# Differential heads' values and probabilities as plain float32, the joint's rows one after another, later residual loads and earlier weight sums in a decoder layer

## The chip, the cores and the metric

One Trainium2 chip, one of its cores. The metric is the device time of one execution in microseconds (us), as the median of several runs. PE is TensorE, DVE is VectorE, ACT is ScalarE, POOL is GpSimd, and SP is the engine whose queue issues every DMA of this kernel.

## The reference, cut to what matters

One decoder layer over 1024 tokens and 1024 channels, all float32. A common input projection feeds 4 differential heads and 8 sparse ("NSA") heads; both results go through one output projection, a first layer norm, a SwiGLU feed-forward of width 2816 and a second layer norm.

```python
s = einsum('bqhcd,bkhcd->bhcqk', q_blk, k) * scale - slopes * dist     # two score maps, c = 0, 1
p = masked_softmax(s, dist >= 0)
a = p[:, :, 0] - lam * p[:, :, 1]
o_diff = einsum('bhqk,bkhe->bqhe', a, v)                              # v has 128 columns per head
mix = concatenate([o_diff, o_nsa]) @ w_out
x = layer_norm(ALPHA * x + mix, ln1_g, ln1_b)
ffn = (silu(x @ w_gate) * (x @ w_up)) @ w_down
x = layer_norm(ALPHA * x + ffn, ln2_g, ln2_b)
```

## The kernel before, in words

**Numbers in two halves.** A float32 matrix product is made of products of the type float32r. An operand is split into a high part (ACT casts it, L80) and a low part (DVE or POOL subtracts, L82); `mm3` (L115 to L117) adds high-high, high-low and low-high products into one PSUM bank of 512 columns. Transpositions on PE (L329, L483, L848) and the small products of the compression (L206) are plain float32.

**Attention.** Work is cut into units: one head (differential) or head pair (NSA) and one block `i` of 128 queries, so a unit has `i + 1` blocks of 128 keys. A unit's *front* makes scores on PE (L303, L304) into one of two PSUM banks `psS`, DVE scales them and takes the row's extreme (L307), ACT takes the exponential (L320), and DVE (L443 to L446) and POOL (L448, L449) combine the two maps. Its *back* transposes the result (L329) in groups of up to four blocks into `psT`, splits each group into high and low parts (`pt`, L80 and L82) and multiplies it with the values (L462, L464) into the only bank `psO`. The values of a differential head lie as 256 columns, high and low beside each other; each of the two products takes all 256, so the result has two halves of 128 columns, which ACT copies (L468) and DVE adds (L469); ACT squares the sum (L470). After four units `finish` scales the rows, transposes them (L483), and writes them to `mix_d` in DRAM (L486, L488).

**Fillers.** The table `phases` puts projections (`qf`, `kf`, `qdf`, `kdf`, `dvf`), weight loads (`wo_fill`) and the first output rows (`out_fill`) between the units; `pump` gives them out in proportion to the units' cost. `dvf(pair, blocks)` makes the values of two heads; for pair 1 it stands in the phases of heads 0 and 1. A scheduler then orders each engine's instructions by these priorities and by its own idea of what is ready. Engines work in that order, one instruction behind the other.

**The joint.** Output rows 4 to 7 (`out_half_now`, two halves of 24 products) and their layer norms run between attention and feed-forward. `x_put` transposes a finished row block and splits it into the feed-forward's moving operands; `x_sums(i)` forms the sums and differences (L864, L865, L867) of blocks `i - 4` and `i` for a seven-product scheme. The order is written out by hand: half 0 of rows 6 and 7, half 1 of row 6, the norm of row 6, half 1 of row 7, and so on. The norm takes DVE, POOL and ACT in turn, except for row 7, which is on DVE but for the root.

**Gate, up and down.** Eleven steps `p` of a pair of gate tiles and a pair of up tiles, 7 x 12 products each. `hidden_operands(p)` writes seven combinations of the hidden rows to `a_d`, `down_weights(p)` reads two weight rows into slots 11 and 9, forms four combinations on DVE and writes seven blocks to `t_d`. `down_weights(p - 1)` is called in step `p`, and that of the last pair after the loop. The down projection then runs seven passes (numbers 1, 2, 6, 5, 3, 7, 4) over 11 operands. `down_operand` loads each from `a_d` and `t_d` (L1051, L1052) into one of 16 places, and splits it; an operand serves 12 products. `residual` (L1073) loads the rows of the first norm back from `x1_d`, and `norm_params(ln2)` (L596) the second norm's scale and shift.

Of the kernel before, what the change touches and what calls it, by code (L numbers as in the profile page):

```python
# [11 lines left out]
F32 = mybir.dt.float32  # L12
F32R = mybir.dt.float32r
# [4 lines left out]
P = 128  # L18
# [20 lines left out]
def layer_kernel(ctx: ExitStack, tc: tile.TileContext, xT, x, w_t, w_vg, w_dv, lam_in, subln,  # L39
# [103 lines left out]
    with ExitStack() as ctx_a:  # L143
# [177 lines left out]

        def pt_tile():
            return pa.tile([P, 1024], F32R, tag="pt", name="pt", bufs=3)

# [99 lines left out]
        def diff_units(h, qt, kd, V):  # L424
# [3 lines left out]
            def make(i):  # L428
# [22 lines left out]
                def back(fill):  # L451
                    if i4 == 0:
                        state["orow"] = small([P, 4, P], "od", 2)
                        state["ss"] = small([P, 4], "ss", 2)
                    orow, ss = state["orow"], state["ss"]
                    po = ps_o()
                    for j4 in range(0, i + 1, 4):
                        js = range(j4, min(j4 + 4, i + 1))
                        pt = transposed([ts[0][:, j * P:(j + 1) * P] for j in js])
                        for n, j in enumerate(js):  # L460
                            v = V[j // 2][:, (j % 2) * 512 + (h % 2) * 256:(j % 2) * 512 + (h % 2 + 1) * 256]
                            nc.tensor.matmul(po[:, :256], lhsT=pt[:, 0, n * P:(n + 1) * P], rhs=v,  # L462
                                             start=(j == 0), stop=False)
                            nc.tensor.matmul(po[:, :256], lhsT=pt[:, 1, n * P:(n + 1) * P], rhs=v,  # L464
                                             start=False, stop=(j == i))
                        fill((j4 + len(js)) / (i + 1))
                    tmp = small([P, P], "ms", 2)
                    nc.scalar.copy(tmp, po[:, 128:256])  # L468
                    nc.vector.tensor_add(orow[:, i4, :], po[:, 0:128], tmp)  # L469
                    nc.scalar.activation(tmp, orow[:, i4, :], AF.Square, accum_out=ss[:, i4:i4 + 1])  # L470
                    if i4 == 3:
                        late.append(lambda: finish(orow, ss, state["r0", hf]))
# [57 lines left out]

        def dv_fill(pair, where, out, blocks):
            def steps():
                parts = [(*load_split(w_dv[pair, :, kk, :], *w_tiles(), l_eng="pool", pieces=2), 4 * kk, 4) for kk in range(2)]
                for i in blocks:
                    if i % 2 == 0:
                        out.append(slot(where[i // 2]))
                    ps = ps_m()
                    yield from proj_rows(parts, 256, i, ps)
                    dst = out[i // 2][:, (i % 2) * 512:(i % 2 + 1) * 512].rearrange("p (h s e) -> p h s e", h=2, s=2)
                    split(ps[:, :256].rearrange("p (h e) -> p h e", h=2), dst[:, :, 0, :], dst[:, :, 1, :])  # L540
            return steps, 2.61 * len(blocks)
# [50 lines left out]

        def norm_params(src):
            lnp[:] = [slot(0, F32), slot(1, F32)]
            for n in range(2):
                nc.sync.dma_start(lnp[n], src[n].unsqueeze(0).to_broadcast([P, DM]))  # L596
# [137 lines left out]
        def dvf(pair, blocks):  # L734
            return dv_fill(pair, ((8, 9, 10, 11), (6, 7, 3, 5))[pair], vd[pair], blocks)

# [6 lines left out]
        def held_fill():  # L743
# [15 lines left out]
            (diff(0), [qdf(0, 1), dvf(1, range(4)), qdf(1, 0)], 1, 0, 1),  # L759
            (diff(1), [qdf(1, 1), dvf(1, range(4, 8)), kdf(2, 0), kdf(2, 1), qdf(2, 0)], 1, 0, 1),  # L760
            (diff(2, 0, 4), [kdf(3, 0), kdf(3, 1), qdf(3, 0)], 0, 0, 2),
            (diff(3, 0, 4), [qdf(2, 1)], 0, 0, 2),
            (diff(2, 4), [wo_fill(0), qdf(3, 1), wo_fill(1), held_fill(), out_fill(0, False), out_fill(1, False)], 0, 0, 2),
# [126 lines left out]
    for i in (6, 7):  # L890
        out_start(i)
        out_half_now(i, 0, ps_s())
    x_sums(5)
    X["22"] = (x_big(), x_big())
    out_half_now(6, 1, ps_m())
    norm1(6)
    for i in (4, 5):
        x_put("22", i, acc[i][:, HI])
    out_half_now(7, 1, ps_m())
    x_sums(6)  # L900
    norm1(7, vector_only=True)
    x_put("22", 6, acc[6][:, HI])

# [95 lines left out]
    for p in range(NF // 2):  # L999
# [3 lines left out]
        next(gate)  # L1003
        if p == 0:
            x_sums(7)
            X["T1"] = (x_big(), x_big())
            next(up)
        next(gate)
# [10 lines left out]
        if p > 0:  # L1019
            next(up)  # L1020
            down_weights(p - 1)
        next(up)
# [166 lines left out]
```

## Time and profile before

| | |
|---|---|
| runs | median 1359.04 us, 1359.03 to 1361.04, of 3 |
| the profiled execution | 1355.88 us, of which the span is 1354.2 us |
| TensorE clock granted | 0.991 of full |
| busy | PE 97%, weight loads 83%, DVE 70%, ACT 48%, POOL 35% |
| DMA | 184.17 MB, 136 GB/s over the span |

A row of the timeline has start, duration, engine, line, operation and operands; what stands in brackets is how long the engine was idle before it and who ended that. A row of the windows has, for a stretch of the span, the busy time and number of instructions of each engine, the granted clock (1.00 is full), the share of the DMA engines and GB/s. Products are pipelined and their ends are modelled: a product's row can be longer than the distance to the next one's start, which is called the pitch below. A plain float32 product shows as two rows.

### The profile page before, as it was taken

What the parts mean: (1) busy time and instruction counts of PE and PEld (TensorE: products, weight loads), DVE (VectorE), ACT (ScalarE), POOL (GpSimd) and SP (SyncE); (2) the same over time, 40 slices, a digit from 0 to 9 for tenths busy, and PEclk for the clock granted to TensorE, in tenths of its full rate; (3) what the DMA queues carried; (4) which work ended last, traced back from release to release, by engine and by line L of the source; (5) the groups of instructions that cost most, each with busy time, mean ns of one, the idle gap of its engine ahead of it and who ended that gap; (6) DMA issues with size and microseconds to landing.
All of it is one profiled execution on the core that took longest, in us unless ns stands there. A gap on an engine that the chain in (4) does not pass through costs nothing.

```text
span 1354.2 us, 20369 instructions
## 1 busy us (share of the span) xinstructions
PE 1312.3 (97%) x7018; PEld 1121.8 (83%) x7018; DVE 946.6 (70%) x1936; ACT 649.9 (48%) x1329; POOL 475.2 (35%) x468
## 2 busy tenths in 40 slices
PE   8999999999999999799989999999999999899997
PEld 6898998888899988578867888888888888688886
DVE  5546768778796757874678677767767767555588
ACT  5336567677686656743336233333333325443330
POOL 5415244343543636633631233322322322000071
PEclk9999999999999999999989999999999999999999
DMA  9312021120203226423212655545555559765641
GB/s 360 123 26 61 7 59 49 30 63 16 72 15 83 79 55 197 131 79 133 101 63 86 203 193 180 179 164 187 170 172 191 190 210 400 276 217 189 199 169 65
DMA packets 87271, 184.17 MB, mean 136 GB/s; under 512 B 10624, under 2 KB 19200, under 8 KB 87040
## 3 DMA queue, kind: packets, MB, share of 16 engines
q1 hardware_dynamic: 87168, 182.87, 41.3%
q8 instruction: 55, 0.90, 0.3%
q14 instruction: 48, 0.39, 0.1%
HBM read 117.23 MB, written 57.15 MB: 129 GB/s over the span
## 4 chain that ended last, share of the span: by engine, by line
PE 85%; DMA 6%; DVE 5%; ACT 2%; issue 1%; SPq 0%; POOLq 0%; DVEq 0%; POOL 0%; ACTq 0%
PE psM L115 10%; PE psM L116 10%; PE psM L117 9%; PE psT L329 5%; PE psS L115 5%; PE psT L115 5%; PE psS L117 5%; PE psT L117 5%; PE psS L116 5%; PE psT L116 5%; PE psS L303 3%; PE psS L304 3%; PE psO L408 2%; PE psO L406 2%; DMA big<-t_d 2%; PE psO L115 2%
## 5 line engine op out<-in xcount | busy, mean ns | idle before, releaser
L320 ACT ACTIVATE t<-t,m 128x128 f32<-128x128 f32 (+7 forms) x192 | 144.3, 752 | 52.9 <-DVE m L307 47.2
L391 POOL TENSOR_SCALAR t<-t,r,gates 128x640 f32<-128x640 f32 (+7 forms) x128 | 100.6, 788 | 156.3 <-DVE r L390 103.4
L82 DVE TENSOR_TENSOR pt<-psT,pt 128x512 fp32r<-128x512 f32 (+2 forms) x200 | 117.8, 599 | 20.0 <-ACT pt L80 18.3
L115 PE MATMUL psM<-big,w 128*128 128x512 f32 x304 | 122.6, 403 | 3.0 <-ACT w L80 2.8
L80 ACT CAST pt<-psT 128x512 fp32r<-128x512 f32 (+2 forms) x200 | 99.9, 518 | 47.7 <-PE psT L329 22.0
L116 PE MATMUL psM<-big,w 128*128 128x512 f32 x304 | 120.7, 397 | 0.0
L117 PE MATMUL psM<-big,w 128*128 128x512 f32 x304 | 120.4, 397 | 0.0
L303 PE MATMUL psS<-slot,q 128*128 128x320 f32 (+5 forms) x288 | 106.5, 371 | 8.4 <-DVE m L307 7.3
L329 PE MATMUL psT<-ident,t 128*128 128x128 f32 x672 | 107.9, 274 | 2.3 <-ACT tmp L486 1.6
L957 POOL TENSOR_TENSOR half<-half,half 128x512 f32<-128x512 f32 x22 | 32.2, 1462 | 218.5 <-ACT half L956 218.5
L304 PE MATMUL psS<-slot,q 128*128 128x320 f32 (+5 forms) x288 | 95.6, 333 | 0.0
L329 PEld LDWEIGHTS psT<-ident,t 128*128 128x128 f32 x672 | 80.1, 141 | 9.8 <-ACT tmp L486 2.1
L307 DVE CUSTOM_DVE_ANT_0 t<-psS,dsel 128x512 f32<-128x512 f32 (+5 forms) x128 | 68.3, 535 | 27.5 <-PE psS L304 24.3
L82 DVE TENSOR_TENSOR op<-op 128x1024 fp32r<-128x1024 f32 x44 | 62.7, 1432 | 35.1 <-ACT op L80 34.8
L82 DVE TENSOR_TENSOR big<-slot,big 128x1024 fp32r<-128x1024 f32 (+1 forms) x53 | 64.7, 1231 | 32.1 <-ACT big L80 32.1
L80 ACT CAST big<-slot 128x1024 fp32r<-128x1024 f32 (+1 forms) x53 | 54.1, 1034 | 54.9 <-DVE slot L949 46.4
L80 ACT CAST op<-op 128x1024 fp32r<-128x1024 f32 x44 | 45.9, 1050 | 58.1 <-DMA op<-t_d 51.9
L80 ACT CAST big<-big 128x1024 fp32r<-128x1024 f32 (+1 forms) x49 | 44.6, 913 | 57.3 <-DMA big<-t_d 47.0
L408 PE MATMUL psO<-pt,slot 128*128 128x256 f32 x264 | 71.6, 293 | 0.3 <-DVE pt L82 0.2
L406 PE MATMUL psO<-pt,slot 128*128 128x256 f32 x264 | 71.1, 287 | 0.0
L303 PEld LDWEIGHTS psS<-slot,q 128*128 128x128 f32 x288 | 54.7, 190 | 18.5 <-DVE m L307 14.2
L115 PEld LDWEIGHTS psM<-big,w 128*128 128x128 f32 x304 | 57.7, 190 | 14.1 <-ACT w L80 3.6
(364 smaller groups left out, 3970.9 us busy)
## 6 DMA issues: line engine op xcount, KB each, us to landing
a_d<-slot SPq DMA_DIRECT2D x77, 256.0 KB, 3.0
t_d<-slot SPq DMA_DIRECT2D x77, 256.0 KB, 2.3
q<-q SPq DMA_DIRECT2D x48, 256.0 KB, 3.0
slot<-in_w_up_dram SPq DMA_DIRECT2D x22, 512.0 KB, 3.8
slot<-in_w_down_dram SPq DMA_DIRECT2D x22, 512.0 KB, 4.3
op<-a_d SPq DMA_DIRECT2D x44, 256.0 KB, 3.3
op<-t_d SPq DMA_DIRECT2D x44, 256.0 KB, 3.6
big<-a_d SPq DMA_DIRECT2D x33, 256.0 KB, 2.9
```

Of the source, the lines that this page charges most:

```text
L80: nc.scalar.copy(hi, src)
L82: eng.tensor_sub(lo, src, hi.bitcast(F32))
L115: nc.tensor.matmul(acc, lhsT=ah, rhs=bh, start=first, stop=False, skip_group_check=more)
L116: nc.tensor.matmul(acc, lhsT=ah, rhs=bl, start=False, stop=False, skip_group_check=more)
L117: nc.tensor.matmul(acc, lhsT=al, rhs=bh, start=False, stop=last, skip_group_check=more)
L303: nc.tensor.matmul(ps[:, :w], lhsT=q[0], rhs=k[:, ks], start=True, stop=False)
L304: nc.tensor.matmul(ps[:, :w], lhsT=q[1], rhs=k[:, ks], start=False, stop=True)
L320: nc.scalar.activation(t[:, :width], t[:, :width], AF.Exp, bias=m, scale=-1.0, accum_out=r)
L329: nc.tensor.transpose(tp[:rows, n * P:(n + 1) * P], s, ident)
L391: nc.gpsimd.tensor_scalar(ts[a][:, :width], ts[a][:, :width], r[:, a:a + 1], gates[:, i, gc:gc + 1], op0=ALU.mult, op1=ALU.mult)
L406: nc.tensor.matmul(po[:, :256], lhsT=v, rhs=pt[:, 0, n * 256:(n + 1) * 256], start=False, stop=False)
L408: nc.tensor.matmul(po[:, :256], lhsT=v, rhs=pt[:, 1, n * 256:(n + 1) * 256], start=False, stop=last)
```

## The change

1. **Differential heads.** `transposed_whole` copies each group of transposed probabilities once (ACT, L332 of the kernel after) to float32. The values stay whole: `dv_fill` copies them with ACT alone, four blocks to a slot. One float32 product of 128 columns (L472) takes the place of L462 and L464. DVE copies the result (L476) and ACT squares it straight from PSUM (L477).
2. **Values of pair 1.** They need two slots, not four; the weights are loaded once and lie in the slots 10, 11, 3 and 5. `dvf(1, range(4, 8))` moves from the phase of head 1 to that of the first half of head 3.
3. **Joint.** Row 6 is made whole, then its norm starts, then row 7 is made whole. `x_put("22", 4 to 6)` comes after row 7's norm. In step 0 the up tile's first part is written ahead of `x_sums(7)`.
4. **Weight sums.** `down_weights(p)` is called in step `p`; step 2 makes those of 0 and 2, and nothing is left after the loop.
5. **Residual loads.** `not_before` copies one column (DVE) of a bank's evacuated sum into the tile that is to be loaded, so that the load waits for the pass before; so also for the second norm's parameters.

```diff
-                        pt = transposed([ts[0][:, j * P:(j + 1) * P] for j in js])
+                        pt = transposed_whole([ts[0][:, j * P:(j + 1) * P] for j in js])
                         for n, j in enumerate(js):
-                            nc.tensor.matmul(po[:, :256], lhsT=pt[:, 0, n * P:(n + 1) * P], rhs=v,
-                                             start=(j == 0), stop=False)
-                            nc.tensor.matmul(po[:, :256], lhsT=pt[:, 1, n * P:(n + 1) * P], rhs=v,
-                                             start=False, stop=(j == i))
+                            c = (j % 4) * 256 + (h % 2) * P
+                            nc.tensor.matmul(po[:, :P], lhsT=pt[:, n * P:(n + 1) * P], rhs=V[j // 4][:, c:c + P],
+                                             start=(j == 0), stop=(j == i))
...
-                    nc.scalar.copy(tmp, po[:, 128:256])
-                    nc.vector.tensor_add(orow[:, i4, :], po[:, 0:128], tmp)
-                    nc.scalar.activation(tmp, orow[:, i4, :], AF.Square, accum_out=ss[:, i4:i4 + 1])
+                    nc.vector.tensor_copy(orow[:, i4, :], po[:, :P])
+                    nc.scalar.activation(tmp, po[:, :P], AF.Square, accum_out=ss[:, i4:i4 + 1])
...
-            (diff(1), [qdf(1, 1), dvf(1, range(4, 8)), kdf(2, 0), kdf(2, 1), qdf(2, 0)], 1, 0, 1),
+            (diff(1), [qdf(1, 1), kdf(2, 0), kdf(2, 1), qdf(2, 0)], 1, 0, 1),
-            (diff(3, 0, 4), [qdf(2, 1)], 0, 0, 2),
+            (diff(3, 0, 4), [qdf(2, 1), dvf(1, range(4, 8))], 0, 0, 2),
...
     for i in (6, 7):
         out_start(i)
-        out_half_now(i, 0, ps_s())
+    for nh in range(2):
+        out_half_now(6, nh, ps_s())
     x_sums(5)
-    out_half_now(6, 1, ps_m())
     norm1(6)
-    out_half_now(7, 1, ps_m())
+    for nh in range(2):
+        out_half_now(7, nh, ps_m())
     x_sums(6)
...
         if p > 0:
             next(up)
-            down_weights(p - 1)
+            if p == 2:
+                down_weights(0)
+            down_weights(p)
...
+    def not_before(src, *tiles):
+        for t in tiles:
+            nc.vector.tensor_copy(t[:, 0:1], src[:, 0:1])
-    def residual(i, t):
+    def residual(i, t, after):
         acc[i] = t
+        not_before(after, t)
         nc.sync.dma_start(t, x1_d[i])
```

**What moves, place one: PE at the joint.** Rows of PE's order before, from the end of the first gate and up products on the operand `x11` on; `half` is a difference that `x_sums` made, and the number tells which:

```order
L117 MATMUL psS<-x11h,big 128x512
L117 MATMUL psO<-x11h,big 128x512
L115 MATMUL psO<-x11h,big 128x512
L116 MATMUL psO<-x11l,big 128x512
L117 MATMUL psO<-x11h,big 128x512
L848 MATMUL psT<-ident,half_8452 128x128 x4
L115 MATMUL psS<-x21h,big 128x512
```

And of the kernel after, the end of row 7's last half (`psM`) and what follows:

```order
L117 MATMUL psM<-big,w 128x512
L862 MATMUL psT<-ident,half_8174 128x128 x4
L862 MATMUL psT<-ident,half_8175 128x128 x4
L862 MATMUL psT<-ident,slot_7790 128x128 x4
L862 MATMUL psT<-ident,slot_7800 128x128 x4
L862 MATMUL psT<-ident,slot_8018 128x128 x4
L115 MATMUL psS<-x11h,big 128x512
L116 MATMUL psS<-x11l,big 128x512
```

The differences of row 6 (`half_8452` before, `half_8174` after) stood behind the `x11` products and now stand ahead of them, right behind row 7's 48 products.

**Place two: SP's queue in the down projection.** A stretch of the queue before, early in the pass; `x_d` is `x1_d`, and `slot_11394` holds a block of the last hidden rows:

```order
L1051 DMA big<-a_d 128x512
L1052 DMA big<-t_d 128x512
L1073 DMA w<-x_d 128x1024
L991 DMA a_d<-slot_11394 128x512
L1073 DMA w<-x_d 128x1024
L1051 DMA big<-a_d 128x512
L1073 DMA slot_11892<-x_d 128x1024
```

The first residual loads of the kernel after, which stand behind the loads of 26 operands:

```order
L1066 DMA big<-a_d 128x512
L1067 DMA big<-t_d 128x512
L1094 DMA slot_11624<-x_d 128x1024
L1094 DMA slot_11628<-x_d 128x1024
L1094 DMA slot_11632<-x_d 128x1024
L1066 DMA op<-a_d 128x512
```

All eight residual loads stood among the first pass's operands; now four stand behind its operands and four more 23 operands later.

**Place three: PE among the wide units of head 2.** Before, the last units of head 2 (`slot_6358` holds keys):

```order
L464 MATMUL psO<-slot_5679,pt 128x256
L303 MATMUL psS<-slot_6358,q 128x512
L304 MATMUL psS<-slot_6358,q 128x512
L303 MATMUL psS<-slot_6358,q 128x512
L304 MATMUL psS<-slot_6358,q 128x512
L462 MATMUL psO<-slot_5521,pt 128x256
```

After, the same scores (`slot_6045` holds the keys):

```order
L115 MATMUL psM<-big,w 128x512
L472 MATMUL psO<-slot_5500,pt 128x128 x4
L303 MATMUL psS<-slot_6045,q 128x512
L304 MATMUL psS<-slot_6045,q 128x512
L116 MATMUL psM<-big,w 128x512
L117 MATMUL psM<-big,w 128x512
L303 MATMUL psS<-slot_6045,q 128x512
L304 MATMUL psS<-slot_6045,q 128x512
```

Products of the output projection (`psM`) now stand between scores that followed each other.

More of the change, by code (lines that the diff above doesn't have):

```diff
@@ L320, in exps, with pt_tile, transposed_whole @@
             nc.scalar.activation(t[:, :width], t[:, :width], AF.Exp, bias=m, scale=-1.0, accum_out=r)
-        def pt_tile():
-            return pa.tile([P, 1024], F32R, tag="pt", name="pt", bufs=3)
+        def pt_tile(dt=F32R):
+            return pa.tile([P, 1024], dt, tag="pt", name="pt", bufs=3)
+        def transposed_whole(srcs):
+            tp = ps_t()
+            for n, s in enumerate(srcs):
+                nc.tensor.transpose(tp[:, n * P:(n + 1) * P], s, ident)
+            w = len(srcs) * P
+            pt = pt_tile(F32)
+            nc.scalar.copy(pt[:, :w], tp[:, :w])
+            return pt
         def transposed(srcs, rows=P):
@@ L529, in q_fill, with dv_fill @@
             return steps, 5.2
-        def dv_fill(pair, where, out, blocks):
+        dv_parts = {}
+        def dv_fill(pair, where, out, blocks, tiles):
             def steps():
-                parts = [(*load_split(w_dv[pair, :, kk, :], *w_tiles(), l_eng="pool", pieces=2), 4 * kk, 4) for kk in range(2)]
+                if pair not in dv_parts:
+                    dv_parts[pair] = [(*load_split(w_dv[pair, :, kk, :], *tiles(kk), l_eng="pool", pieces=2), 4 * kk, 4)
+                                      for kk in range(2)]
+                parts = dv_parts[pair]
                 for i in blocks:
-                    if i % 2 == 0:
-                        out.append(slot(where[i // 2]))
+                    if i % 4 == 0:
+                        out.append(slot(where[i // 4], F32))
                     ps = ps_m()
                     yield from proj_rows(parts, 256, i, ps)
-                    dst = out[i // 2][:, (i % 2) * 512:(i % 2 + 1) * 512].rearrange("p (h s e) -> p h s e", h=2, s=2)
-                    split(ps[:, :256].rearrange("p (h e) -> p h e", h=2), dst[:, :, 0, :], dst[:, :, 1, :])
+                    nc.scalar.copy(out[i // 4][:, (i % 4) * 256:(i % 4 + 1) * 256], ps[:, :256])
             return steps, 2.61 * len(blocks)
@@ L591, in out_fill, with norm_params @@
             return steps, 10.4
-        def norm_params(src):
+        def norm_params(src, after=None):
             lnp[:] = [slot(0, F32), slot(1, F32)]
+            if after is not None:
+                not_before(after, *lnp)
             for n in range(2):
@@ L734, in dvf @@
         def dvf(pair, blocks):
-            return dv_fill(pair, ((8, 9, 10, 11), (6, 7, 3, 5))[pair], vd[pair], blocks)
+            tiles = [lambda kk: w_tiles(), lambda kk: [slot(n) for n in ((10, 11), (3, 5))[kk]]][pair]
+            return dv_fill(pair, ((8, 9), (6, 7))[pair], vd[pair], blocks, tiles)
         held = []
@@ L891, in layer_kernel @@
         out_start(i)
-        out_half_now(i, 0, ps_s())
+    for nh in range(2):
+        out_half_now(6, nh, ps_s())
     x_sums(5)
-    X["22"] = (x_big(), x_big())
-    out_half_now(6, 1, ps_m())
     norm1(6)
-    for i in (4, 5):
-        x_put("22", i, acc[i][:, HI])
-    out_half_now(7, 1, ps_m())
+    for nh in range(2):
+        out_half_now(7, nh, ps_m())
     x_sums(6)
     norm1(7, vector_only=True)
-    x_put("22", 6, acc[6][:, HI])
+    X["22"] = (x_big(), x_big())
+    for i in (4, 5, 6):
+        x_put("22", i, acc[i][:, HI])
     turns = {"banks": 0, "gate": 0}
@@ L1004, in layer_kernel @@
         if p == 0:
+            next(up)
             x_sums(7)
             X["T1"] = (x_big(), x_big())
-            next(up)
         next(gate)
@@ L1028, in layer_kernel @@
         hidden_operands(p, g)
-    down_weights(NF // 2 - 1)
     A_AT = {1: 0, 2: 1, 4: 2, 5: 3, 6: 4, 7: 5, 3: 6}
@@ L1084, in layer_kernel @@
         nc.scalar.copy(us[j], bs[j])
-        residual(j, slot((2, 4, 3, 6)[j], F32))
+        residual(j, slot((2, 4, 3, 6)[j], F32), us[j])
     down(2, bs, True)
@@ L1092, in layer_kernel @@
         nc.vector.tensor_add(us[j], bs[j], us[j])
-        residual(j + 4, w_tile(F32))
-    norm_params(ln2)
+        residual(j + 4, w_tile(F32), us[j])
+    norm_params(ln2, us[3])
     bs = banks()
```

1 line of the change is left out of this document (removed).

## The prediction

> **What bounds the kernel now.** First the page's head and the waits of PE, longest first (engine, operand, line, whom it waited for, us in total, times, longest).
>
> ```profile
> span 1354.2 us, 20369 instructions
> PE 1312.3 (97%) x7018; PEld 1121.8 (83%) x7018; DVE 946.6 (70%) x1936; ACT 649.9 (48%) x1329; POOL 475.2 (35%) x468
> ...
> PE psS L303 <- DVE m L307: 7.3, 16, 1.6
> PE psT L848 <- DVE half L865: 5.3, 1, 5.3
> ...
> PE psS L115 <- ACT op L80: 1.6, 1, 1.6
> ```
>
> PE is the bound: a change gains what it takes off PE's stream, or off PE's waits. The longest single one is the joint's (L848), and the sixteen for L307 are short; where they lie the windows show (busy time of PE, weight loads, DVE, ACT and POOL, then clock, DMA share and GB/s).
>
> ```profile
> 490.00:520.00 30.00, 29.58 (x163) 25.22 (x162) 20.39 (x61) 17.34 (x48) 12.20 (x12) 1.00 0.28 81
> ...
> 540.00:550.00 10.00, 6.64 (x31) 4.71 (x30) 7.19 (x20) 9.49 (x26) 8.49 (x9) 0.95 0.92 296
> 550.00:560.00 10.00, 7.73 (x39) 6.44 (x38) 7.03 (x26) 5.38 (x20) 6.85 (x8) 0.88 0.37 80
> 560.00:570.00 10.00, 8.44 (x53) 6.77 (x52) 9.32 (x30) 7.82 (x22) 4.34 (x5) 1.00 0.17 54
> 570.00:585.00 15.00, 10.72 (x64) 8.46 (x63) 11.38 (x36) 8.81 (x24) 6.99 (x7) 0.94 0.38 124
> ...
> 690.00:700.00 10.00, 6.42 (x29) 4.94 (x27) 9.93 (x15) 2.19 (x3) 6.06 (x4) 0.96 0.10 25
> 700.00:710.00 10.00, 7.13 (x23) 5.50 (x24) 5.17 (x9) 2.88 (x5) 2.90 (x2) 0.53 0.34 134
> ...
> 1150.00:1160.00 10.00, 5.80 (x26) 4.48 (x25) 5.26 (x5) 4.98 (x6) 0.00 (x0) 1.00 1.05 399
> 1160.00:1170.00 10.00, 10.00 (x39) 8.11 (x38) 8.15 (x9) 4.09 (x5) 0.00 (x0) 0.83 0.82 286
> ```
>
> These are head 1, where PE hardly waits (490 to 520), heads 2 and 3 (540 to 585), the joint (690 to 710) and the start of the down projection (1150 to 1170). The idle shown is less than what is lost, because a product's row is longer than its pitch. For the true loss I set the products against their pitch; in the timeline of PE:
>
> ```profile
> 55.95 7.30 PE L206 MATMUL psM<-slot,slot 128*128 128x128 f32 x64
> 63.01 0.38 PE L116 MATMUL psT<-t,big 128*128 128x280 f32 x1
> ...
> 580.08 0.34 PE L303 MATMUL psS<-slot,q 128*128 128x384 f32 x1
> 580.25 0.34 PE L304 MATMUL psS<-slot,q 128*128 128x384 f32 x1
> ...
> 632.07 0.28 PE L464 MATMUL psO<-slot,pt 128*128 128x256 f32 x1
> 632.19 0.28 PE L462 MATMUL psO<-slot,pt 128*128 128x256 f32 x1
> ...
> 642.67 0.39 PE L116 MATMUL psM<-big,w 128*128 128x512 f32 x1
> 642.90 0.39 PE L117 MATMUL psM<-big,w 128*128 128x512 f32 x1
> ...
> 708.38 0.63 PE L116 MATMUL psS<-x21l,big 128*128 128x512 f32 x1
> 708.81 0.63 PE L117 MATMUL psS<-x21h,big 128*128 128x512 f32 x1
> ```
>
> The pitch of a float32r product is 0.23 us at 512 columns, 0.12 at 256 and 0.17 at 384. The 64 rows of L206 are 32 plain float32 products of 128 columns: 7.06 us to the next start, 0.11 a row. The last two rows are the joint at half clock: 0.43 instead of 0.23.
>
> The groups of PE between 540 and 585 say how much work stood there (L304 and L464 are the second products of L303 and L462, as many again; 21 products in all were of L115 to L117).
>
> ```profile
> L303 PE MATMUL psS<-slot,q 128*128 128x384 f32 (+3 forms) x28 | 11.1, 398 | 4.7 <-DVE m L307 4.6
> L462 PE MATMUL psO<-slot,pt 128*128 128x256 f32 x30 | 8.7, 313 | 0.2 <-DVE od L469 0.2
> L329 PE MATMUL psT<-ident,t 128*128 128x128 f32 x36 | 5.7, 276 | 1.6 <-ACT tmp L486 1.6
> L115 PE MATMUL psM<-big,w 128*128 128x512 f32 x7 | 4.0, 575 | 2.9 <-ACT w L80 2.8 <-DVE q L176 0.2
> L483 PE MATMUL psT<-ident,od 128*128 128x128 f32 x8 | 1.3, 286 | 2.1 <-DVE od L480 2.0
> ```
>
> At the pitch: 56 scores x 0.17 + 60 x 0.12 + 44 transpositions x 0.11 + 21 x 0.23 = 26.4 us of work in 45 us, so about 18 are lost (an estimate: the scores' mean width is taken as 384, and a transposition like a row of L206). At the joint the two windows show 3.6 + 2.9 = 6.5 us idle, 12 products at half clock cost 12 x 0.20 = 2.4 more, and I put 2 for ends hidden under rows and for the slow start of what follows: 11 lost. From 1150 to 1170 the windows count 65 products x 0.23 = 15 of 20 us, so 5 are lost; the wait of 1.6 us for an operand comes after 1170, and with 1 for what hides there it is about 7.5.
>
> **The change, part by part.**
>
> *Products of the differential heads.* 36 pairs of blocks in each of 4 heads: 144 times L462 and L464, 0.24 us together, become one float32 product, two rows of 0.11. That is 0.22, so 144 x 0.014 = 2.0 us less on PE. The nearest rows set the ends: 0 if the gain drowns in rounding, 3 if a row costs 0.109 like a transposition. What stands behind L206 starts in step (63.01 closes the 64th row), so changing between the types costs nothing that these rows show. [...]
>
> *What leaves DVE and ACT.* Each group loses its subtraction:
>
> ```profile
> L82 DVE TENSOR_TENSOR pt<-psT,pt 128x512 fp32r<-128x512 f32 (+2 forms) x200 | 117.8, 599 | 20.0 <-ACT pt L80 18.3
> ```
>
> The differential heads have 12 groups each, 48 in all, some 25 us of DVE at up to 0.6 each; the copy L468, ahead of the add, goes too. All of this lies beside PE, and counts only where PE waits for DVE, which is 540 to 585.
>
> *Heads 2 and 3.* There PE starves: units with little filler, scores that wait for L307 to free a bank, DVE 34.9 of 45 us busy. Into this stretch come the four blocks of `dvf(1, 4..7)`: 4 x 24 products x 0.12 = 11.5 us of PE work that no unit waits for soon. They take the place that the last query projection and the first output rows had, and these move on between head 2's wide units (place three). DVE loses some 12 groups, 7 us, and its chain per unit is 0.6 us shorter. 11.5 us of filler alone can hide at most 11.5 of the 18. One wait stays: the first output row needs heads 2 and 3, whose result goes through DRAM, and its split stands ahead of the next unit in DVE's order, now as before.
>
> ```profile
> 583.33 0.69 DVE L82 TENSOR_TENSOR w<-w 128x512 fp32r<-128x512 f32 x1 [3.31 <-ACT w L80]
> ```
>
> That is 3 us of PE again. I leave another 3 for waits too short to name: 18 - 6 = 12 gained. Ends: 4 (only DVE's relief shows) and 16 (all but the last wait's rest goes). The filler is missing in head 1's phase. There PE had 0.4 us idle in 30 and DVE 20.4 busy, so DVE alone would not bind it with 10 us less on PE in some 70; I charge 1.5 us, ends -2 and 6, which also stand for the new order of the sparse heads.
>
> *Joint.* Before, row 6's norm began two halves (48 products) later than it could, and the differences that it yields stood in PE's order behind the `x11` products with nothing else to do. DVE's timeline:
>
> ```profile
> 667.44 0.68 DVE L578 SCALAR_TENSOR_TENSOR slot<-slot,psM 128x512 f32<-128x512 f32 x1
> ...
> 678.78 0.69 DVE L865 TENSOR_TENSOR half<-slot 128x512 f32<-128x512 f32 x1
> ...
> 684.70 0.68 DVE L578 SCALAR_TENSOR_TENSOR slot<-slot,psM 128x512 f32<-128x512 f32 x1
> ...
> 700.88 0.68 DVE L865 TENSOR_TENSOR half<-slot 128x512 f32<-128x512 f32 x1
> ```
>
> The first two rows are row 5's norm, from its last sum to the end of the difference: 12.0 us. The last two are row 6's, 16.9 us, with row 7's own norm (L609, L611) in between on DVE. Now row 6 has row 7's 48 products (48 x 0.23 = 11 us) and two groups of transpositions as cover, so 12 us of norm end as PE arrives: at most 1 us of wait. Then five groups of transpositions follow each other with three banks `psT`, and DVE must empty each in 0.6 us among the norm of row 7: about 1 us. The first gate products then need a low part (L82, 1.2 us) that stands behind two steps of that norm of 0.6 each: 2 us. Sum 4, each under what halved the clock at 700. Gain 11 - 4 = 7; ends 4 and 10.
>
> *Down.* The DMA engines are full (share 1.05, 399 GB/s) up to 1160, and PE idles 4.2 us for the first operand of the third pass. Among its predecessors are the residual loads:
>
> ```profile
> slot<-x_d SPq DMA_DIRECT2D x4, 512.0 KB, 5.8
> w<-x_d SPq DMA_DIRECT2D x4, 512.0 KB, 6.1
> ...
> 1157.80 0.33 SPq L974 DMA_DIRECT2D slot<-in_w_down_dram  x1
> 1164.72 0.37 SPq L977 DMA_DIRECT2D t_d<-slot  x1
> ```
>
> 8 x 512 KB are 4.2 MB, at 400 GB/s 10 us of a full queue, and that goes behind the first pass; so do 1 MB of norm parameters. The two last rows are the last pair's weight sums: loaded at 1157.80, written at 1164.72, and only then can the first pass's last operand be read, for which PE waits the 1.6 us. That chain now ends a step, some 38 us of gate and up, earlier (14 sets of 12 products x 0.23). The added wait: SP holds everything behind L1094 until ACT has evacuated a bank, but 26 operands are issued ahead of it, of which PE has used 11; the 27th finds no free place before the pass ends anyway. With 15 operands ahead, 15 x 12 x 0.23 = 41 us, four loads of 1.3 us each hide. The ten 1-column copies on DVE lie beside PE, as nobody needs those tiles soon. Step 2's second `down_weights` adds 4 operations of 0.6 us on DVE in a step of 38. 7.5 - 0.5 = 7 gained; ends 3 (the queue stays full with operands) and 8.
>
> *Sum.* 2 + 12 + 7 + 7 - 1.5 = 26.5 us. The profiled execution took 1355.88, so 1329.4; the runs' median lies 3.2 us above it, so 1359.0 - 26.5 = 1332.5.
>
> **The rivals.**
>
> *The units of heads 2 and 3 keep their pace* because their latency and not missing filler sets it: ACT is 9.49 of 10 us busy at 540, and that stays. For it: scores wait for L307 sixteen times; against it: DVE and ACT are far from full after 550. Then 4 instead of 12: 1340.5.
>
> *The joint's wait returns*: row 6's norm takes 17 us, as it did with row 7's on the same engine. The wait is then 5 us and the clock halves again: only 1 gained there, 1338.5.
>
> *Slower: ACT stands behind late weights.* The second half of the output weights comes in four pairs of loads, and ACT's casts of them stand in its order ahead of head 2's exponentials. The group from 540 to 584:
>
> ```profile
> L80 ACT CAST big<-big 128x512 fp32r<-128x512 f32 x8 | 5.1, 633 | 2.5 <-DMA big<-wo_d 2.5
> ```
>
> If each of the eight casts waits the 2.5 us that one of them did, that is 20 us, and if the clock then halves as at 700, 10 more: 1359.0 - 26.5 + 30 = 1362.5. It turns the sign where each wait is over 2.3 us. Against it: all eight together waited 2.5.
>
> *Nothing moves*: PE's waits only change their names, as PE is 97% busy by the page; against it speaks the loss by pitch, 37 us in three places. 1359.
>
> **How the numbers follow.** Forecast 0.58, heads 2 and 3 0.17, joint 0.12, slower 0.05, nothing 0.04, and 0.04 that all upper ends meet (1319 and less). The likeliest gives 1332.5. The ends of the terms are apart by 3, 12, 8, 6 and 5 us; as they are unlikely to fall together, I take about 13 us to each side, 1319 to 1346, which holds the first three cases. A difference of 0.2% (2.7 us) is about what a measurement can tell from none: faster 0.58 + 0.17 + 0.12 + 0.04 = 0.91, same 0.04, slower 0.05.
>
> **What would show it.** The steps are right if L472's rows follow each other at 0.11, the wait for `half` at the joint is under 1.5 us and no window there shows a clock near 0.5, no operand of the down projection is waited for over 1 us, and PE is over 85% busy in each window of heads 2 and 3 but the one with the mix row. They are wrong if L472 runs at 0.12 or more a row, if a new wait of several us stands in the sparse heads or head 1, or if the first down operands still come late at a DMA share over 1.

## The result, and the profile after

| | before | after |
|---|---|---|
| runs, median (lowest to highest) | 1359.03 us (1358.83 to 1361.04), 4 | 1337.86 us (1335.19 to 1338.85), 3 |
| ratio of the times | | 0.9837, 95% interval 0.9816 to 0.9858 |
| the profiled execution, its span | 1355.88 us, 1354.2 us | 1335.19 us, 1333.5 us |

A fourth run of the kernel after took 1447.95 us at a granted clock of 0.85 and is left out (with it the median is 1338.36). The change takes 21.2 us off (1359.03 - 1337.86), and 20.7 between the two profiled executions, where 26.5 were forecast. First PE's waits of the kernel after (engine, operand, line, whom it waited for, us in total, times, longest):

```profile
PE psS L303 <- DVE m L307: 5.4, 12, 0.7
...
PE psM L115 <- ACT w L80: 2.0, 2, 1.2
PE psS L303 <- DMA q<-q: 1.7, 1, 1.7
PE psS L117 <- DVE big L82: 1.5, 2, 1.2
...
PE psT L862 <- DVE xT3l L82: 0.8, 1, 0.8
```

The 5.3 us wait for `half` is gone, and so are both waits for operands of the down projection. The windows at the places that the prediction speaks of (PE, weight loads, DVE, ACT, POOL, clock, DMA share, GB/s):

```profile
490.00:520.00 30.00, 28.05 (x171) 24.08 (x170) 19.46 (x65) 21.72 (x57) 17.59 (x19) 1.00 0.24 78
...
540.00:550.00 10.00, 10.00 (x71) 9.31 (x70) 6.80 (x25) 5.42 (x19) 4.09 (x6) 1.00 0.41 120
550.00:560.00 10.00, 10.00 (x59) 8.68 (x57) 5.48 (x15) 7.16 (x16) 5.92 (x5) 1.00 1.00 360
560.00:570.00 10.00, 9.65 (x50) 7.37 (x49) 7.57 (x26) 7.58 (x19) 10.00 (x10) 1.00 0.51 128
570.00:585.00 15.00, 12.42 (x76) 10.38 (x76) 10.24 (x35) 9.59 (x24) 6.26 (x6) 1.00 0.32 105
...
690.00:700.00 10.00, 8.85 (x39) 7.35 (x40) 10.00 (x15) 4.34 (x7) 0.00 (x0) 1.00 0.28 107
700.00:710.00 10.00, 10.00 (x58) 8.23 (x57) 5.62 (x9) 4.65 (x8) 1.30 (x1) 1.00 0.37 131
...
1150.00:1160.00 10.00, 10.00 (x46) 8.29 (x45) 2.10 (x2) 2.75 (x3) 0.00 (x0) 1.00 1.01 358
1160.00:1170.00 10.00, 10.00 (x46) 8.29 (x45) 6.47 (x6) 5.59 (x6) 0.00 (x0) 1.00 0.57 187
```

Heads 2 and 3 are full but for the stretch with the mix row (570 to 585), the clock stays whole at the joint, and the down projection starts without a gap at a DMA share that is still 1.01. Head 1 (490 to 520) has lost 1.5 us more than before.

A row of 512 columns lasts 0.39 us where the next one starts after 0.23, so windows hide losses below a row's length. I therefore set each PE row against its pitch in every profile: the distance to the next row's start, less 0.227 us for 512 columns, 0.204 for 448, 0.176 for 384, 0.147 for 320, 0.118 for 256, 0.111 for a plain float32 row of 128 and 0.109 for a transposition. The sums of what is over (us, by stretches of each kernel's own span):

| kernel | 0-220 | 220-360 | 360-440 | 440-520 | 520-600 | 600-760 | 1120-end | all |
|---|---|---|---|---|---|---|---|---|
| before | 11.4 | 7.4 | 3.4 | 2.5 | 20.6 | 12.9 | 8.3 | 66.0 |
| after | 11.1 | 9.5 | 8.4 | 4.0 | 9.6 | 5.8 | 0 | 47.6 |
| after_again | 10.3 | 9.7 | 8.5 | 4.0 | 12.1 | 5.8 | 0 | 50.0 |
| part1_alone | 10.4 | 9.4 | 8.5 | 0.9 | 13.8 | 12.7 | 6.9 | 62.0 |
| parts345 | 11.4 | 7.4 | 3.4 | 2.5 | 18.1 | 5.8 | 0 | 47.8 |
| dvf_back | 10.5 | 10.0 | 8.5 | 0.9 | 15.6 | 7.4 | 0 | 52.0 |
| dvf_half | 10.3 | 10.0 | 8.4 | 1.0 | 15.0 | 5.8 | 0 | 49.7 |
| w_first | 10.3 | 9.2 | 3.6 | 8.2 | 7.8 | 7.4 | 0 | 45.7 |
| w_first_again | 10.5 | 9.1 | 3.6 | 8.2 | 7.4 | 5.8 | 0 | 43.7 |
| w_half | 11.0 | 9.1 | 3.6 | 5.2 | 17.8 | 5.8 | 0 | 51.7 |
| w_back | 10.7 | 9.2 | 3.6 | 3.2 | 17.5 | 5.8 | 0 | 49.5 |
| rows_only | 10.4 | 9.9 | 8.5 | 4.0 | 11.7 | 4.0 | 0 | 47.8 |
| res_early | 10.7 | 10.1 | 8.5 | 4.0 | 12.6 | 7.4 | 0 | 52.6 |
| lag | 10.5 | 9.8 | 8.4 | 5.5 | 9.4 | 7.4 | 4.0 | 55.5 |

The kernels below "after" are the experiments. From 760 to 1120 all are within 0.5 us of no loss. Kernels with the same order agree to 0.1 us from 360 to 440 (8.4 or 8.5 in eight of them), and differ by some 3 us in heads 2 and 3 (9.4 to 12.6 in the four profiles after, after_again, res_early and lag). From before to after 18.4 us of loss go, and the products take 2.0 less (1277.8 us at their pitch before, 1275.8 after): 20.4 of the 20.7 between the two profiles. Where the forecast and this differ most is one place: from 220 to 440, in the sparse heads, 7 us have *come*.

### The profile page after: what moved, and what is told of

It reads as the page before. It is cut to its first block, busy times and chain, and to the rows that moved or that the text cites. A ratio compares the mean times of both kernels' runs of the same rounds, so it can differ in the third digit from the quotient of the medians.

```text
span 1333.5 us, 20339 instructions
## 1 busy us (share of the span) xinstructions
PE 1305.0 (98%) x7018; PEld 1116.4 (84%) x7018; DVE 918.9 (69%) x1882; ACT 638.3 (48%) x1293; POOL 468.9 (35%) x464
## 4 chain that ended last, share of the span: by engine, by line
PE 88%; DVE 4%; DMA 3%; ACT 1%; issue 1%; POOL 1%; SPq 0%; POOLq 0%; DVEq 0%; ACTq 0%
PE psM L115 10%; PE psM L117 10%; PE psM L116 10%; PE psT L117 6%; PE psT L115 6%; PE psT L116 6%; PE psS L117 6%; PE psS L115 6%; PE psS L116 5%; PE psT L339 4%; PE psS L303 3%; PE psS L304 3%; PE psO L418 2%; PE psO L472 2%; PE psO L416 2%; PE psO L117 2%
## 5 line engine op out<-in xcount | busy, mean ns | idle before, releaser
L303 PE MATMUL psS<-slot,q 128*128 128x320 f32 (+5 forms) x288 | 106.4, 372 | 7.4 <-DVE m L307 5.4
L971 POOL TENSOR_TENSOR half<-half,half 128x512 f32<-128x512 f32 x22 | 33.3, 1515 | 198.7 <-ACT half L970 198.7
L82 DVE TENSOR_TENSOR pt<-psT,pt 128x512 fp32r<-128x512 f32 (+1 forms) x152 | 91.5, 613 | 12.4 <-ACT pt L80 11.5
L307 DVE CUSTOM_DVE_ANT_0 t<-psS,dsel 128x512 f32<-128x512 f32 (+5 forms) x128 | 67.7, 535 | 34.1 <-PE psS L304 30.2
L80 ACT CAST pt<-psT 128x512 fp32r<-128x512 f32 (+1 forms) x152 | 76.8, 527 | 26.5 <-PE psT L339 14.1
L339 PE MATMUL psT<-ident,t 128*128 128x128 f32 x528 | 83.8, 273 | 1.5 <-DVE pt L82 1.3
L418 PE MATMUL psO<-pt,slot 128*128 128x256 f32 x264 | 73.2, 298 | 0.7 <-DVE pt L82 0.6
L975 POOL TENSOR_TENSOR half<-half,half 128x512 f32<-128x512 f32 x22 | 36.4, 1657 | 101.8 <-DVE half L974 101.7
L303 PEld LDWEIGHTS psS<-slot,q 128*128 128x128 f32 x288 | 54.4, 189 | 17.7 <-DVE m L307 12.9
L339 PEld LDWEIGHTS psT<-ident,t 128*128 128x128 f32 x528 | 62.5, 140 | 7.7 <-issue 1.4
L115 PEld LDWEIGHTS psM<-big,w 128*128 128x128 f32 x304 | 57.2, 188 | 12.6 <-ACT w L80 2.7
```

Of the source, the lines that this page charges most:

```text
L80: nc.scalar.copy(hi, src)
L82: eng.tensor_sub(lo, src, hi.bitcast(F32))
L115: nc.tensor.matmul(acc, lhsT=ah, rhs=bh, start=first, stop=False, skip_group_check=more)
L303: nc.tensor.matmul(ps[:, :w], lhsT=q[0], rhs=k[:, ks], start=True, stop=False)
L339: nc.tensor.transpose(tp[:rows, n * P:(n + 1) * P], s, ident)
L418: nc.tensor.matmul(po[:, :256], lhsT=v, rhs=pt[:, 1, n * 256:(n + 1) * 256], start=False, stop=last)
```

## The experiments

The theory after the result: the 7 us are filler that the sparse heads miss, since `dvf(1, 4..7)` moved to head 3. The rival: they come from the whole values themselves.

**The moved blocks put back** (dvf_back, against the changed kernel).

```diff
-            (diff(1), [qdf(1, 1), kdf(2, 0), kdf(2, 1), qdf(2, 0)], 1, 0, 1),
+            (diff(1), [qdf(1, 1), dvf(1, range(4, 8)), kdf(2, 0), kdf(2, 1), qdf(2, 0)], 1, 0, 1),
-            (diff(3, 0, 4), [qdf(2, 1), dvf(1, range(4, 8))], 0, 0, 2),
+            (diff(3, 0, 4), [qdf(2, 1)], 0, 0, 2),
```

> The changed kernel, but with the values of blocks 4 to 7 of pair 1 back in the phase of head 1. Theory: the 7 us that PE loses more from 220 to 440 (18.0 us of stalls, 10.8 before) are missing filler, because these 11.5 us of products used to be drawn forward into the sparse heads' last units. Then PE's stalls from 220 to 440 fall back to 11 +- 2, heads 2 and 3 (520 to 600) lose 8 to 10 of their gain of 11, and the time is 1340 to 1343 against 1338.4. Rival: the loss comes from the whole values themselves (ACT's copies and two more weight slots change the order of the sparse heads); then the stalls from 220 to 440 stay at 17 to 19 and the time is 1346 to 1349.

1337.48 us (1336.20 to 1339.45), ratio 0.9852 (0.9833 to 0.9871). The loss from 360 to 440 stays at 8.5 and that from 220 to 360 at 10.0: the theory falls, the rival's loss is there. But the rival's time is not: heads 2 and 3 lose 15.6 instead of 9.6 to 12.1, and head 1 gets 3.1 back (4.0 to 0.9), so that the move as it stands pays 0 to 3 us by the pitch, and nothing that the times show (1337.48 against 1337.86).

**Part 1 alone** (part1_alone): the changed kernel with the joint's block, `down_weights`, the residual loads and the phases as before. The new slots of pair 1's values and weights, which part 2 names, stay in it.

> The kernel before with part 1 alone: whole float32 values and probabilities in the differential heads, pair 1's weights loaded once, nothing else. Theory: 2 us from the products and about 3 to 4 us in heads 2 and 3 from DVE's missing subtractions, nothing lost in the sparse heads: 1353 to 1355 against 1359.0. Rival (whole values disturb the sparse heads): the same 5 to 6 gained and 7 lost there, 1359 to 1361.

1350.53 us (1349.00 to 1358.32), ratio 0.9953 (0.9938 to 0.9967): 7.1 us faster, more than either side expected. Its loss from 220 to 440 is 17.9, as after. So whole values, together with these slots, cost the sparse heads 7 us; which of the two it is, this run does not tell. In heads 2 and 3 the loss falls from 20.6 to 13.8 with no filler added there.

**Parts 3, 4 and 5 alone** (parts345): the kernel before with the new joint, `down_weights(p)` in step `p` and the held residual loads.

> The kernel before with the three late parts alone: the joint's rows in sequence, the weight sums in their own pair, the residual loads held back; values and probabilities in halves as before, in their old phases. Theory: the stages are independent, so the joint's 7.1 us and the down projection's 8.5 us come off whole: 1343 to 1344 against 1359.0, with the stalls up to 680 as before. Rival: an earlier end of attention shifts what the joint finds ready, and the joint keeps its wait here: 1349 to 1351.

1340.60 us (1337.71 to 1344.07), ratio 0.9873 (0.9853 to 0.9892). The joint and the down projection give their whole gain by themselves (12.9 to 5.8 and 8.3 to 0), and the sparse heads are as before. These three parts are worth 17.1 us, and parts 1 and 2 together only the rest. Part 1 with its slots gives 3.1 us on top of them (dvf_back, 1337.48, in the same set of runs), where alone it gave 7.1; why the two do not add up is not shown. Heads 2 and 3 lose 18.1 here in the order of before, which lost 20.6, so 2.5 us there can be chance.

**Half of the blocks put back** (dvf_half: `dvf(1, range(4, 6))` in head 1's phase, `range(6, 8)` in head 3's).

> The changed kernel, but with blocks 4 and 5 of pair 1 back in the phase of head 1, and 6 and 7 in that of the first half of head 3. Theory (stalls fall where filler is, by 1.5 to 2 us for each 20 us that had none): half of the 7 us in the sparse heads come back and about half of the 8 us in heads 2 and 3 go: 1338 to 1341. Rival: the last units of the sparse heads need only a few products to be covered, and 5.7 us of filler are enough for them while the other half is enough for heads 2 and 3: 1333 to 1336.

1338.24 us (1337.41 to 1338.74), ratio 0.9857 (0.9837 to 0.9878). In time the theory's 1338 to 1341, but not by its way: the sparse heads do not move, and heads 2 and 3 stay at 15.0.

What holds the sparse heads up can then be read in the trace. In the kernel after, the timelines of PE, ACT and POOL around the values of pair 1:

```profile
370.18 0.28 PE L116 MATMUL psM<-slot,big 128*128 128x256 f32 x1
...
371.37 0.28 PE L117 MATMUL psM<-slot,big 128*128 128x256 f32 x1
405.57 0.39 PE L115 MATMUL psM<-slot,big 128*128 128x256 f32 x1
...
406.98 0.28 PE L117 MATMUL psM<-slot,big 128*128 128x256 f32 x1
...
418.23 1.14 ACT L80 CAST slot<-w 128x512 fp32r<-128x512 f32 x2
...
422.48 2.51 POOL L82 TENSOR_TENSOR slot<-w,slot 128x512 fp32r<-128x512 f32 x2
...
424.89 0.28 PE L116 MATMUL psM<-slot,big 128*128 128x256 f32 x1
```

The first half of a block (12 products, over four k-tiles) runs at 370, that of a second block at 405, and then but two products (at 419.6) until 425: the second half needs weights that are cast at 418 and split at 422. They go to slots 3 and 5, and these hold values of the sparse heads (`V = ((2, 3), (4, 5))`), which the sparse heads' last units still read: PE's last product on such values (L418) runs from 421.88 to 422.16, and the split starts at 422.48. The projection that used to fill the sparse heads' end thus waits for that end.

**The first four blocks' weights in passing tiles** (w_first, against the changed kernel).

```diff
-                if pair not in dv_parts:
-                    dv_parts[pair] = [(*load_split(w_dv[pair, :, kk, :], *tiles(kk), l_eng="pool", pieces=2), 4 * kk, 4)
-                                      for kk in range(2)]
-                parts = dv_parts[pair]
+                parts = [(*load_split(w_dv[pair, :, kk, :], *tiles(kk), l_eng="pool", pieces=2), 4 * kk, 4)
+                         for kk in range(2)]
...
-            tiles = [lambda kk: w_tiles(), lambda kk: [slot(n) for n in ((10, 11), (3, 5))[kk]]][pair]
+            early = blocks[0] == 0
+            tiles = (lambda kk: w_tiles()) if early else lambda kk: [slot(n) for n in ((10, 11), (3, 5))[kk]]
```

> The changed kernel, but the first four blocks of pair 1's values take their weights in the passing weight tiles, as before, and only the later four load them again into slots 10, 11, 3 and 5. Theory: slots 3 and 5 hold the sparse heads' values until their last unit, so in the changed kernel the second half of the weights is cast at 418 and split at 425, and the products on them can't be drawn forward; with other tiles they stand among the units from 367 on, PE's stalls from 360 to 440 fall from 8.4 to 3.4 +- 1, and the time is 4 to 5 us under the changed kernel beside it. Rival: the stalls come from the order that ACT's copies of whole values give, or from the scheduler's picture of shorter products; then 360 to 440 stays over 7, and the time is within 2 us of the changed kernel or, with 1 MB more to load and split, above it.

As the measure beside it the changed kernel ran again, with no edit (after_again).

> The changed kernel once more, unchanged, beside the three kernels sent with it, as their measure: 1335 to 1339, and PE's stalls per stretch within 0.5 us of the first profile (360 to 440: 8.4; 520 to 600: 9.6, where 2 us either way may come from DMA).

1337.40 us (1335.73 to 1337.54), ratio 0.9852 (0.9835 to 0.9868) for the changed kernel, and 1333.42 us (1331.25 to 1334.68), ratio 0.9824 (0.9806 to 0.9842) for w_first: 4.0 us less. In w_first the weights are there early, and both halves of the blocks run among the units:

```profile
360.33 1.13 ACT L80 CAST w<-w 128x512 fp32r<-128x512 f32 x2
361.49 2.52 POOL L82 TENSOR_TENSOR w<-w 128x512 fp32r<-128x512 f32 x2
...
369.84 0.28 PE L115 MATMUL psM<-w,big 128*128 128x256 f32 x1
...
373.74 0.28 PE L117 MATMUL psM<-w,big 128*128 128x256 f32 x1
401.39 0.38 PE L115 MATMUL psM<-w,big 128*128 128x256 f32 x1
```

and the one window from 360 to 440, of the kernel before, of the kernel after, and of w_first:

```profile
360.00:440.00 80.00, 79.45 (x576) 73.69 (x575) 65.55 (x209) 58.46 (x140) 36.78 (x41) 1.00 0.23 58
```

```profile
360.00:440.00 80.00, 77.59 (x559) 70.14 (x558) 72.14 (x236) 63.37 (x155) 42.35 (x47) 1.00 0.16 42
```

```profile
360.00:440.00 80.00, 79.45 (x564) 73.13 (x563) 62.47 (x201) 58.55 (x139) 38.00 (x43) 1.00 0.23 58
```

PE is as busy as before the change, and the loss is 3.6 again: the slots are the cause of 5 of the 7 us. The 2 us from 220 to 360 stay (9.2, 7.4 before); they come with the whole values in every kernel, and why stays open. Part of the gain is lost again in head 1, where the filler is then spent (4.0 to 8.2).

**Residual loads early again** (res_early): `not_before(after, t)` left out of `residual`, and `norm_params(ln2)` without its `after`; the data that the loads bring are the same.

> The changed kernel without the copies that hold the residual loads and the second norm's parameters back; the weight sums stay in their own pair. As the prediction has it, both edits share the down projection's 8.5 us: 4 MB of residuals and 1 MB of parameters among the first pass's operands keep the DMA engines full up to 1160, and the 4.4 us wait for the third pass's first operand comes back: 4 to 5 us over the changed kernel. Rival: only the late weight sums made the operands late, and the residual loads hide: within 1 us of the changed kernel.

1337.73 us (1335.01 to 1340.13), ratio 0.9856 (0.9837 to 0.9876), against 1337.40 of the changed kernel beside it, as the rival had it. The windows of res_early at the start of the down projection:

```profile
1130.00:1140.00 10.00, 10.00 (x46) 8.29 (x45) 9.38 (x10) 5.27 (x5) 0.03 (x1) 1.00 1.05 399
1140.00:1150.00 10.00, 10.00 (x46) 8.29 (x45) 3.68 (x3) 4.32 (x6) 0.00 (x0) 1.00 1.04 403
```

The DMA engines are as full as before the change (1.05, 399 GB/s), and PE does not wait at all.

**Weight sums a step late again** (lag).

```diff
-            if p == 2:
-                down_weights(0)
-            down_weights(p)
+            down_weights(p - 1)
...
         hidden_operands(p, g)
+    down_weights(NF // 2 - 1)
```

> The changed kernel, but with each pair's weight sums a step late again and the last pair's after the loop; the residual loads stay held back. As the prediction has it, the last pair's sums reach memory too late for the first pass's last operand, and PE waits 1.8 to 4 us about 26 operands into the down projection: 2 to 4 us over the changed kernel. Rival: without the residual loads the DMA engines have room, the sums arrive in time, and it is within 1 us.

1343.24 us (1342.08 to 1344.50), ratio 0.9898 (0.9881 to 0.9914): 5.8 us over the changed kernel, more than the theory's 2 to 4. Its windows:

```profile
1140.00:1150.00 10.00, 7.70 (x34) 5.80 (x32) 6.72 (x6) 5.25 (x5) 0.00 (x0) 0.99 0.97 350
1150.00:1160.00 10.00, 10.00 (x38) 8.05 (x38) 6.85 (x9) 5.16 (x5) 0.00 (x0) 0.84 0.89 301
```

A wait of 2.3 us and a lowered clock behind it (0.84 over 10 us), 4.0 us by the pitch. Beside after_again this profile also loses 1.6 more at the joint, where its clock fell (0.83 from 690 to 700), 1.5 more in head 1 and 2.7 less in heads 2 and 3, so 4.0 is what the edit is shown to cost. With both edits undone it is 6.9 to 8.3 (part1_alone, before), with both or the weight sums alone in place 0. So the early weight sums alone remove all of the loss; holding the loads back only halves it where the sums are late. SP's rows of the last pair's last weight load and of its last sums show by how much the chain moved; before:

```profile
1157.80 0.33 SPq L974 DMA_DIRECT2D slot<-in_w_down_dram  x1
...
1170.14 0.98 SPq L983 DMA_DIRECT2D t_d<-slot  x2
```

and after:

```profile
1086.94 0.33 SPq L988 DMA_DIRECT2D slot<-in_w_down_dram  x1
...
1093.25 3.22 SPq L997 DMA_DIRECT2D t_d<-slot  x3
```

71 us earlier, of which 12 are the lead that the kernel has by then; the prediction counted one step of 38.

**Three more, beside w_first once more** (w_first_again, no edit).

> The kernel w_first once more, as the measure for the two beside it: 1331 to 1335.

1331.47 us (1330.62 to 1333.82), ratio 0.9805 (0.9787 to 0.9824). In w_half blocks 4 and 5 stand in head 1's phase (`early = blocks[0] < 6`), in w_back all four (all weights in `w_tiles()`).

> Like w_first, but blocks 4 and 5 of pair 1's values stand in the phase of head 1 (weights in the passing tiles), and only 6 and 7 in that of the first half of head 3. Theory: PE's stalls follow the filler; the 8.2 us from 440 to 520 in w_first, where 6 us of filler stand in 20, fall to 3 to 5, and heads 2 and 3 rise from 7.8 to 10 to 12: the same time within 2 us. Rival: heads 2 and 3 need all four blocks and go back to 15 as in dvf_half: 4 us slower than w_first.

> Whole values and the three late parts, but pair 1's weights in the passing tiles for both calls and all four late blocks in the phase of head 1, as before: neither the move nor the slots. If the move pays once the slots are out of the way, this is 3 to 5 us slower than w_first (stalls of 15 in heads 2 and 3, 1 to 3 from 440 to 520); if the move only carries stalls from one stretch to the other, it is within 2 us of w_first.

1338.49 us (1337.55 to 1341.99; ratio 0.9859, 0.9839 to 0.9879) and 1336.92 us (1336.18 to 1339.46; ratio 0.9846, 0.9827 to 0.9865). Both lose over 17 in heads 2 and 3, where w_first_again loses 7.4. That is the rival of w_half, and more than its 4 us (7.0 over w_first_again). The move pays 5.5 us (w_back less w_first_again), a little over the 3 to 5 expected, once the slots are out of the way. Heads 2 and 3 do not take the filler in proportion: half of it there (dvf_half, w_half) gave nothing.

**Only the order of the rows at the joint** (rows_only).

```diff
     x_sums(5)
+    X["22"] = (x_big(), x_big())
     norm1(6)
+    for i in (4, 5):
+        x_put("22", i, acc[i][:, HI])
     for nh in range(2):
         out_half_now(7, nh, ps_m())
     x_sums(6)
     norm1(7, vector_only=True)
-    X["22"] = (x_big(), x_big())
-    for i in (4, 5, 6):
-        x_put("22", i, acc[i][:, HI])
+    x_put("22", 6, acc[6][:, HI])
...
         if p == 0:
-            next(up)
             x_sums(7)
             X["T1"] = (x_big(), x_big())
+            next(up)
```

> The changed kernel with only the rows of the joint in sequence: the operands x22 of rows 4 and 5 are written ahead of row 7 and row 6's behind its norm as before, and the up tile's first part stands behind the sums of row 7 again. By the prediction the order of the rows does the work, because row 6's norm gets row 7's 48 products as cover: PE's stalls from 680 to 760 stay at 5 to 7, the wait for a difference of row 6 under 1.5 us, 1337 to 1339. Rival: the other two moves keep DVE free for row 6's norm; without them the wait is back at 3 us or more, the clock halves, stalls are 9 to 12 and the time is 1341 to 1345.

1335.10 us (1332.15 to 1339.44), ratio 0.9831 (0.9807 to 0.9854). PE's waits of this kernel at the joint, all of them (its lines behind the block are numbered one higher):

```profile
PE psT L862 <- DVE half L881: 1.0, 2, 0.7
PE psT L862 <- DVE half L879: 0.5, 1, 0.5
PE psS L115 <- ACT half L971: 0.3, 1, 0.3
PE psS L117 <- DVE big L82: 0.3, 1, 0.3
```

The order of the rows does the work: 4.0 us of loss from 600 to 760, against 5.8 or more with the other two moves, and the wait for `xT3l` is gone, that for the low part `big` down to 0.3. So those two moves cost 1.8 us in the profile; in the times the difference is inside the spread.

## Why the prediction was right or wrong

The direction, the size (21.2 of 26.5 us) and the range held. One term failed, one was right for a reason that was half wrong, and the rest came near. By the first profile the terms add up to 2.0 + 11.0 + 7.1 + 8.3 - 8.3 = 20.1 us; the same program's second profile (after_again) is 2.4 us worse by the pitch, so how near the sum came is in part luck. Step by step:

*Products of the differential heads, 2.0 forecast: 2.0.* PE's timeline of the kernel after, between two full products:

```profile
566.06 0.40 PE L115 MATMUL psM<-big,w 128*128 128x512 f32 x1
566.30 1.05 PE L472 MATMUL psO<-slot,pt 128*128 128x128 f32 x8
567.11 0.48 PE L303 MATMUL psS<-slot,q 128*128 128x512 f32 x1
567.42 0.39 PE L304 MATMUL psS<-slot,q 128*128 128x512 f32 x1
```

From 566.30 to 567.42 are 1.12 us; less L303's own 0.23 that leaves 0.89 for eight rows, 0.111 each, 0.22 a product.

*Heads 2 and 3, 12 forecast: 8.5 to 11.0* (20.6 to 12.1 and 9.6 in the two profiles). The size nearly held; the split behind it is less sure. I counted DVE's relief as the lower end, 4; part 1 alone gave 6.8 and dvf_back kept 5.0, but against the 18.1 of parts345, whose order there is that of before, these are 4.3 and 2.5. The moved blocks add 3.5 to 6 where the forecast gave them 8, and 3.1 of that is given back in head 1 (0.9 to 4.0).

*Missing filler, 1.5 charged, ends -2 and 6: 8.3* (7.1 from 220 to 440, 1.5 in head 1, 0.3 back ahead of 220). This is the step that failed, 6.8 us beyond its charge and outside its ends; the down projection's 1.3 more made up for a part. The sign named for it, a new wait of several us, did not show: the longest single wait that PE has from 220 to 520 is 0.7 us, and the loss came in many short ones. I looked for the lost filler only where the diff took it out of the table of phases. The weights' new slots, which part 2 names, did more: slots 3 and 5 are in use until the last sparse unit, and the values' products stood ahead of that before, as they do in w_first. 5 us are shown to be theirs (w_first), 2 more in the sparse heads are open; in head 1 the move cost 3.1 (dvf_back), of which part 1 itself had gained 1.6 (2.5 to 0.9).

*Joint, 7 forecast: 7.1.* Row 6's norm, from its last sum to the end of the difference, takes 9.5 us on DVE's timeline of the kernel after, 12 were counted:

```profile
674.56 0.68 DVE L589 SCALAR_TENSOR_TENSOR slot<-slot,psS 128x512 f32<-128x512 f32 x1
...
683.42 0.68 DVE L879 TENSOR_TENSOR half<-slot 128x512 f32<-128x512 f32 x1
```

The waits that were to remain are there by name: 0.8 for `xT3l` in the row of transpositions, 1.2 for the low part of the gate's weights. What failed is "each under what halved the clock", below.

*Down, 7 forecast: 8.3, and half of its argument was wrong.* With the weight sums early, the 4.2 MB of residuals cost nothing (res_early), though they fill the DMA engines (a share of 1.05); the early sums alone bring the whole gain. Only beside late sums do the loads add to the loss (4.0 without them in lag, 6.9 to 8.3 with them). In res_early, from 1130 to 1150, the share is 1.05 and 1.04 and PE waits for nothing, so a share over 1 was no sign of a wait for what is queued. The row at 1164.72 that I read as the sums is a copy of a plain half of a weight row (L977); the last sums are issued at 1170.14 (L983).

The slower rival did not come. The group of ACT's casts of the output weights, from 540 to 585 in the kernel after, waits for them for 0.3 us in all:

```profile
L80 ACT CAST big<-big 128x512 fp32r<-128x512 f32 x8 | 4.8, 626 | 0.3 <-DMA big<-wo_d 0.3
```

Two slips in the arithmetic change no chance: that case turns the sign at 2.2 us a wait (26.5 over 8 waits and half as much again for the clock), not 2.3, and all upper ends together are 39 us, 1320 and not 1319.

## What to carry to other kernels

When a change gives an operand a new place, look up who holds that place and until when; a buffer that is free "by then" can still keep a filler from being drawn forward to where it was of use, which cost 4.0 us here (1337.40 against 1333.42). Parts that share a gain should be toggled one by one: here one of the two edits of the down projection brought the whole gain and the other added nothing to it, and the order of the rows alone brought the joint's. The best kernel of these runs is w_first, 1331.47 and 1333.42 us in two sets of runs (ratios 0.9805 and 0.9824); with the joint of rows_only it might be 2 us less (5.8 to 4.0), which was not tried.

## What the runs showed of the hardware

Short waits can be followed by a halved PE clock too, and not in every run. Ten profiles show the same order and the same waits at the joint to 0.01 us (0.79, 0.13, 0.21 and 1.19 us in a stretch of 5), and in three of them (w_first, res_early, lag) the clock fell behind the last of these (0.91 over 680 to 700, against 1.00 in the other seven). In dvf_back there is a wait of 1.10 us more, and the clock stayed whole (1.00). The windows of w_first, and of w_first_again, the same program in another run:

```profile
685.00:690.00 5.00, 3.59 (x11) 2.37 (x10) 5.00 (x8) 1.98 (x4) 0.00 (x0) 0.80 0.31 105
690.00:695.00 5.00, 5.00 (x20) 3.99 (x20) 5.00 (x9) 2.06 (x4) 0.00 (x0) 0.85 0.27 108
```

```profile
685.00:690.00 5.00, 3.60 (x15) 2.68 (x16) 5.00 (x7) 1.93 (x5) 0.00 (x0) 1.00 0.31 105
690.00:695.00 5.00, 5.00 (x24) 4.14 (x23) 5.00 (x10) 3.09 (x5) 0.00 (x0) 1.00 0.28 110
```

In w_first eight products then follow each other at 0.43 us, 3.4 us in all, which cost 1.6 us; how much of the spread between runs of one kernel comes of this is not shown, nor why the clock fell in three of the ten profiles and not in the other seven.

The clock record of the kernel before has four stretches at half clock ahead of the last 10 us of its span, from 548.93, 583.07, 699.12 and 1159.92 us; they start 34.13, 116.05 and 460.80 us apart, which is 10, 34 and 135 times 3.413. Three of them last 3.413 us and the one at the joint 10.24, three times as long. Their windows:

```profile
548.93:552.34 3.41, 3.41 (x12) 3.02 (x12) 3.30 (x9) 2.02 (x7) 3.30 (x4) 0.50 0.70 149
583.07:586.48 3.41, 3.13 (x10) 2.60 (x11) 3.15 (x8) 3.41 (x8) 0.00 (x0) 0.50 0.01 5
699.12:709.36 10.24, 6.50 (x17) 4.86 (x18) 6.05 (x10) 2.36 (x3) 2.90 (x2) 0.50 0.39 152
1159.92:1163.33 3.41, 3.41 (x9) 2.65 (x9) 2.46 (x3) 1.79 (x3) 0.00 (x0) 0.50 1.04 396
```

Each has a wait of PE just ahead of it or across its start: 1.6 us for L307, 2.8 for `w`, 5.3 for `half` and 4.2 for the third pass's first operand. Its waits of 2.0 us for `od` (until 559.80) and 1.6 for `op` (until 1174.03) have no half clock behind them. The kernel after has one such stretch, from 532.11 us, also of 3.413, behind the wait of 1.7 us for `q`; its 1.2 us wait for `w` and those at the joint have none. How long a wait must be is not shown.
